# A two-layer hybrid block on one core: a fourth weight buffer in the feed-forward, the first mixer without GpSimd, the input also transposed, and an ending by token halves

## The chip, the cores and the metric

The kernel runs on one core of a Trainium2 chip. The metric is the device time in microseconds of one execution. "TensorE" is PE in the profile (PEld is its weight load), VectorE is DVE, ScalarE is ACT, GpSimd is POOL and SyncE is SP.

## The reference

256 tokens of width 2048 pass two layers. Each layer is a mixer and a gated feed-forward, both with a residual and with an RMS norm ahead of them; a last norm follows. Everything is float32.

```
for layer in range(2):
    if layer == 0: h = h + gdn_rglru_mixer(rmsnorm(h, ab_norm), ab_w_in, ...)   # gated delta rule heads + linear recurrence
    else:          h = h + fox_moba_mixer(rmsnorm(h, cd_norm), cd_w_in, ...)    # forgetting attention + block attention
    h = h + (silu(rmsnorm(h, ffn_norm) @ w_gate) * (rmsnorm(h, ffn_norm) @ w_up)) @ w_down   # 2048 -> 5632 -> 2048
return rmsnorm(h, final_norm)
```

In the first mixer `hn @ w_in` gives, for 8 heads of 128, q, k, v and z, two small gate vectors, and the two inputs of an LRU of 8 blocks. q, k, v pass a causal convolution of width 4 and SiLU. The gated delta rule works on chunks of 64 tokens and needs the inverse of a unit lower triangular matrix of each chunk.

## The kernel before

All weights stream once from HBM in units of 128 x 1024 float32 (512 KB). To keep float32 precision at the speed of the one-pass format, each unit is split into a high part (`whi`, a cast on ScalarE, L176) and a low part (`wlo`, a subtraction on VectorE, L177), and the activations `X` are kept as high and low too. A product takes three matmuls: high by high, high by low, low by high. `load` (L160) takes one of three raw buffers and issues the DMA on SyncE; `whi` has four buffers, `wlo` three. `split` (L171) works in steps of `step` columns: 512 in the mixers (`unit`'s default, two ScalarE and two VectorE operations for each unit), 1024 in the feed-forward.

`wstat` (L180) is a projection with the weights as the stationary operand: 2 units, 16 row groups of 128, result transposed (features on partitions); the plain form takes 48 matmuls of 256 columns. `xstat` (L214) has the activations stationary and 512 weight columns moving. `block` (L340) in the feed-forward does a 2 x 2 grid of such outputs, and one group of its row blocks by seven products instead of eight: `seven` loads b11, b12, b22 and b21 and makes sums T1 to T4 of them on VectorE (`total`, L303), so that some raw buffers stay occupied until two sums have read them. A block with four row groups has 12 plain units and 4 loads of this kind. `ffn` (L413) runs 11 gate/up blocks in pieces of 4, 4 and 3, and after each piece two down blocks that add into `h`. `turn` transposes the gated result.

Work beside the projections is written as generators (`tasks`): `tick` after each unit lets up to two of them take a step. So the delta rule's head tasks, the triangular inverse (`group_task`, L670) and the LRU run spread among the projections. The order of instructions on an engine follows the program order, but a tool that lays it out at build time may move ready instructions ahead.

The start: `h` comes in four pieces of 512 KB in natural layout (tokens on partitions), with the first weights between them. `to_x` (L252) transposes it by TensorE, 32 transposes, and ScalarE and VectorE write `X`. Then `mixer0` runs the projections of 8 heads (k, q, v order of the stored weights: L835 on), with the sums of squares of `h` (`sumsq`, L247) after the second tile; `ready` broadcasts the norm factor and starts the gates; the convolutions (`conv`, L490: one multiplication, one ScalarE scaling, three VectorE multiply-adds) follow each projection.

In the first mixer GpSimd does: `vg` (L616, 16 of 128x128), `dec` (L627, 8 of 128x256), the block mask `Cb` (L665, 16 of 128x128), the LRU's products (L559, 8 of 128x256; L578 and L588, 4 each of 128x512), the gating of `ly` (L878, 8 of 128x256), and two memsets. At the end (L1030) it multiplies four pieces by the final norm's weight.

In `group_task` the last step of the inverse works on two pairs of 32-row strips; each pair's result leaves at once:

```
            P2 = ms([128, 8, 32], "Pi4")
            for a, b in pairs:
                for m in range(8):
                    PE.matmul(P2[a, m], V1[b, m], Px[b, m, b], start=True, stop=True)
                V.tensor_scalar_mul(Px[a, :, b], P2[a], -1.0)
```

The end: the last block holds its last three units back, so that token half 0 finishes its matmuls before half 1 (`tail`). `h` is added for both halves, then `last` (L1009) computes the norm of each half, scales it in four pieces and issues four stores for each half on SyncE.

## Time and profile before

| | before |
|---|---|
| median of 3 runs | 2314.95 us (2314.65 to 2317.55) |
| the profiled execution | 2313.76 us |
| its span | 2312.0 us |
| mean granted TensorE clock | 0.997 |
| HBM read | 416.12 MB, mean 181 GB/s over the span |

A row of a stretch (a window) reads: from:to in us, its length, busy us (and number of instructions) of PE, PEld, DVE, ACT and POOL, the granted clock, the DMA engines' mean busy share, GB/s. With one tile's name only the engines that touch the tile are listed. A row of the timeline reads: start, length, engine, line, operation, written tile<-read tiles, size, and in brackets the idle time of the engine ahead of it and what ended it. A row of the groups ends with busy us and mean ns of one, then idle time ahead. A row of the waits reads: who <- for whom: us in total, times, longest. The profile writes some helper tiles short, for instance `F` for the four outputs of a block, `M` for the seven products, `Pi` for the inverse's.

Busy time of TensorE counts matmuls with modelled ends that overlap each other; a matmul of 512 columns is shown with some 0.39 us.

### The profile page before, as it was taken

Reading aid. Unit: us, or ns where it says so; the run is one execution under the profiler, and the core shown is the slowest. Engines: PE = TensorE matmul, PEld = TensorE weight load, DVE = VectorE, ACT = ScalarE, POOL = GpSimd, SP = SyncE. Lnnn points to the kernel's source line nnn. Section 1 sums busy time; section 2 is a strip of 40 time slices with the busy share of each in tenths; the row PEclk is TensorE's granted clock in tenths of the full one; section 3 lists DMA queues with packets and bytes.
Section 4 is the critical chain, followed back from the end, with each engine's and each line's share of the span. In section 5 each row is a group of like instructions: output and inputs, shape, how many; then the busy total and the mean of one; then the engine's idle time right before and its main releaser. Section 6 shows DMA issues by size and latency. Waiting matters only on the chain.

```text
span 2312.0 us, 31583 instructions
## 1 busy us (share of the span) xinstructions
PE 2268.1 (98%) x11630; PEld 1901.1 (82%) x11630; DVE 1824.4 (79%) x2840; ACT 1229.2 (53%) x1826; POOL 58.0 (3%) x74
## 2 busy tenths in 40 slices
PE   8999999999999999999999999999999999999997
PEld 8999888878878888888878888887888878888875
DVE  7898767788787888778876658867888788787888
ACT  7665654555444555455554445545554455554554
POOL 0211200000000000000000000000000000000000
PEclk9999999999999999999999999999999999999999
DMA  6444445566566556666555454555566566566564
GB/s 205 156 157 154 137 146 176 169 192 201 184 191 206 182 192 194 191 199 199 175 188 170 149 171 166 171 189 177 181 200 197 185 194 201 187 199 202 183 209 146
DMA packets 117356, 420.29 MB, mean 182 GB/s; under 512 B 12977, under 2 KB 14513, under 8 KB 117073
## 3 DMA queue, kind: packets, MB, share of 16 engines
q1 hardware_dynamic: 117200, 418.27, 56.0%
q8 instruction: 91, 1.49, 0.3%
q14 instruction: 65, 0.52, 0.1%
HBM read 416.12 MB, written 2.10 MB: 181 GB/s over the span
## 4 chain that ended last, share of the span: by engine, by line
PE 75%; DVE 12%; DMA 8%; ACT 3%; issue 1%; ACTq 0%; DVEq 0%; SPq 0%
PE F L336 13%; PE F L337 12%; PE F L335 12%; PE Pw L192 7%; PE Pw L197 6%; DVE wlo L177 5%; PE Px L237 4%; PE Px L238 4%; PE Px L239 4%; DMA raw<-in_gu 4%; DVE T L306 4%; DMA raw<-in_dn 3%; PE Pw L195 2%; PE Pw L196 2%; ACT whi L176 2%; PE M L337 1%
## 5 line engine op out<-in xcount | busy, mean ns | idle before, releaser
L176 ACT CAST whi<-raw 128x512 fp32r<-128x512 f32 (+1 forms) x1006 | 819.9, 832 | 771.8 <-DMA raw<-in_gu 217.8
L177 DVE TENSOR_TENSOR wlo<-raw,whi 128x512 fp32r<-128x512 f32 (+1 forms) x1006 | 943.7, 955 | 338.4 <-PE F L336 106.6
L336 PE MATMUL F<-wlo,X 128*128 128x512 f32 x1100 | 430.8, 392 | 8.6 <-DVE wlo L177 8.6
L335 PE MATMUL F<-whi,X 128*128 128x512 f32 x1100 | 428.5, 392 | 1.2 <-ACT whi L176 1.1
L337 PE MATMUL F<-whi,X 128*128 128x512 f32 x1100 | 428.5, 390 | 0.0
L197 PE MATMUL Pw<-X,wlo 128*128 128x256 f32 x1152 | 324.2, 282 | 0.0
L336 PEld LDWEIGHTS F<-wlo,X 128*128 128x128 f32 x1100 | 206.6, 188 | 58.3 <-DVE wlo L177 17.2
L335 PEld LDWEIGHTS F<-whi,X 128*128 128x128 f32 x1100 | 206.2, 188 | 44.2 <-ACT whi L176 2.6
L337 PEld LDWEIGHTS F<-whi,X 128*128 128x128 f32 x1100 | 206.5, 188 | 42.7
L192 PE MATMUL Pw<-X,whi 128*128 128x512 f32 x640 | 230.3, 403 | 0.0
L309 ACT CAST thi<-T 128x1024 fp32r<-128x1024 f32 x136 | 142.9, 1051 | 145.5 <-DVE T L306 145.4
L197 PEld LDWEIGHTS Pw<-X,wlo 128*128 128x128 f32 x1152 | 218.7, 190 | 0.4
L336 PE MATMUL F<-wlo,hid 128*128 128x512 f32 x536 | 210.1, 392 | 4.5 <-DVE wlo L177 4.3
L335 PE MATMUL F<-whi,hid 128*128 128x512 f32 x536 | 208.7, 392 | 1.0 <-ACT whi L176 0.9
L337 PE MATMUL F<-whi,hid 128*128 128x512 f32 x536 | 208.9, 390 | 0.0
L310 DVE TENSOR_TENSOR tlo<-T,thi 128x1024 fp32r<-128x1024 f32 x136 | 166.0, 1221 | 28.8 <-ACT thi L309 28.0
L195 PE MATMUL Pw<-X,whi 128*128 128x256 f32 x512 | 148.5, 290 | 0.0
L196 PE MATMUL Pw<-X,whi 128*128 128x256 f32 x512 | 144.9, 283 | 0.0
L192 PEld LDWEIGHTS Pw<-X,whi 128*128 128x128 f32 x640 | 120.2, 188 | 29.3 <-issue 0.7
L336 PEld LDWEIGHTS F<-wlo,hid 128*128 128x128 f32 x536 | 100.6, 188 | 29.7 <-DVE wlo L177 9.4
L335 PEld LDWEIGHTS F<-whi,hid 128*128 128x128 f32 x536 | 100.4, 188 | 22.4 <-ACT whi L176 2.1
L337 PEld LDWEIGHTS F<-whi,hid 128*128 128x128 f32 x536 | 100.6, 188 | 20.5
(357 smaller groups left out, 3217.8 us busy)
## 6 DMA issues: line engine op xcount, KB each, us to landing
raw<-in_gu SPq DMA_DIRECT2D x352, 512.0 KB, 4.2
raw<-in_dn SPq DMA_DIRECT2D x176, 512.0 KB, 4.2
raw<-in_w0w SPq DMA_DIRECT2D x80, 512.0 KB, 3.6
raw<-in_wo SPq DMA_DIRECT2D x64, 512.0 KB, 3.8
raw<-in_w1w SPq DMA_DIRECT2D x64, 512.0 KB, 3.6
raw<-in_w1x SPq DMA_DIRECT2D x32, 512.0 KB, 3.8
raw<-in_w0x SPq DMA_DIRECT2D x16, 512.0 KB, 3.6
h<-in_x SPq DMA_DIRECT2D x4, 512.0 KB, 6.5
```

The costliest lines, as they stand in the source:

```text
L176: S.copy(hi[:, s], raw[:, s])
L177: V.tensor_sub(lo[:, s], raw[:, s], hi[:, s].bitcast(F32))
L192: PE.matmul(P.rearrange("p a b -> p (a b)"), hi[:, kk], X[:, k].rearrange("p a b -> p (a b)"), start=k == 0, stop=False)
L195: PE.matmul(P[:, 0], hi[:, kk], X[:, k, 0], start=k == 0, stop=False)
L196: PE.matmul(P[:, 0], hi[:, kk], X[:, k, 1], start=False, stop=False)
L197: PE.matmul(P[:, 0], lo[:, kk], X[:, k, 0], start=False, stop=k == NK - 1)
L237: PE.matmul(Ps[t], x[:, 0, ts], hi[:, kk], start=k == 0, stop=False)
L309: S.copy(hi, t)
L310: V.tensor_sub(lo, t, hi.bitcast(F32))
L335: PE.matmul(self.t, xh, hi[:, kk], start=self.i == kk == 0, stop=False)
L336: PE.matmul(self.t, xh, lo[:, kk], start=False, stop=False)
L337: PE.matmul(self.t, xl, hi[:, kk], start=False, stop=kk == 1 and self.i == self.n - 1)
```

## The change

1. Feed-forward: every fourth call of `load` takes a buffer `raw4` of its own in the phase's pool, so that four raws rotate.
2. All splits are of 1024 columns.
3. The first mixer's GpSimd operations move to VectorE, the squares `a2` to ScalarE. The memsets stay.
4. The host also passes the input transposed (`xt`). `first` loads it in four quarters, makes `X` from it without TensorE, and runs the first three projections together, quarter by quarter, with weights loaded and split in halves of 512 columns. `h` itself is loaded only after head 1's first projection, where its squares, the norm factor and the LRU rate are computed. Eleven matmuls on zeros come first of all.
5. The convolutions of the first tiles are held in a list; from head 1's third projection on, two are done after each projection. The three outputs of head 0 stay in the PSUM tiles of `ms`.
6. In `group_task` the copies and the scaling of both pairs come after the matmuls of both.
7. At the end the token half 0 is added, normalised, scaled and stored before half 1 is added; three stores for each half (768, 512 and 768 columns), one of them on ScalarE's queue. The last multiplications are VectorE's.

```diff
+    loads, more = [0], []
...
+        more[:] = [] if mixer else [1]
...
-    nc.sync.dma_start(tab[:, 0:NTAB0], A["tab"][:, 0:NTAB0])
-    early = []
-    for g in range(4):
-        nc.sync.dma_start(h[:, :, g * 512:(g + 1) * 512], A["x"][:, :, g * 512:(g + 1) * 512])
...
+    nc.sync.dma_start(col[:, 0:16], A["col"][:, 0:16])
+
+    with tc.tile_pool(name="warm", bufs=1) as wp:
+        wz = wp.tile([128, 256], F32, name="wz")
+        V.memset(wz, 0.0)
+        S.activation(wz[:, 0:1], wz[:, 1:2], AF.Copy)
+        Pz = ms([128, 256], "Pz")
+        for _ in range(11):
+            PE.matmul(Pz, wz[:, 128:256], wz[:, 0:256], start=True, stop=True)
...
     def load(src):
-        if early:
-            return early.pop(0)
-        raw = wr.tile([128, 1024], F32, name="raw")
+        loads[0] += 1
+        if more and loads[0] % 4 == 0:
+            raw = mx.tile([128, 1024], F32, name="raw4", tag="raw4", bufs=1)
+        else:
+            raw = wr.tile([128, 1024], F32, name="raw")
         nc.sync.dma_start(raw, src)
         return raw
...
-        for i in range(0, 1024, step):
-            s = slice(i, i + step)
-            S.copy(hi[:, s], raw[:, s])
-            V.tensor_sub(lo[:, s], raw[:, s], hi[:, s].bitcast(F32))
+        S.copy(hi, raw)
+        V.tensor_sub(lo, raw, hi.bitcast(F32))
         return hi, lo
...
+    def first(srcs, w):
+
+        xt = ogp.tile([128, NK, T], F32, name="xt", tag="og")
+        Ps = [ms([128, T], "Pw") for _ in srcs]
+        for q in range(4):
+            ks, c = slice(4 * q, 4 * q + 4), slice(q % 2 * 512, q % 2 * 512 + 512)
+            nc.sync.dma_start(xt[:, ks], A["xt"][:, ks])
+            if q % 2 == 0:
+                ws = [(wr.tile([128, 1024], F32, name="raw"), wh.tile([128, 1024], F32R, name="whi"),
+                       wl.tile([128, 1024], F32R, name="wlo")) for _ in srcs]
+            for i, (raw, _, _) in enumerate(ws):
+                nc.sync.dma_start(raw[:, c], srcs[i][q // 2][:, c])
+            if q == 0:
+                nc.sync.dma_start(tab[:, 0:NTAB0], A["tab"][:, 0:NTAB0])
+                nc.sync.dma_start(col[:, 16:], A["col"][:, 16:])
+            for k in range(4 * q, 4 * q + 4):
+                S.activation(X[:, k, 0], xt[:, k], AF.Copy, scale=w[:, k:k + 1])
+                V.scalar_tensor_tensor(out=X[:, k, 1], in0=xt[:, k], scalar=w[:, k:k + 1], in1=X[:, k, 0].bitcast(F32),
+                                       op0=ALU.mult, op1=ALU.subtract)
+            for P, (raw, hi, lo) in zip(Ps, ws):
+                S.copy(hi[:, c], raw[:, c])
+                V.tensor_sub(lo[:, c], raw[:, c], hi[:, c].bitcast(F32))
...
-            G.tensor_tensor(out=XI[:, n], in0=XI[:, n], in1=xc, op=ALU.mult)
+            V.tensor_tensor(out=XI[:, n], in0=XI[:, n], in1=xc, op=ALU.mult)
...
-                    G.tensor_tensor(out=a2, in0=R[:, n:n + 2], in1=R[:, n:n + 2], op=ALU.mult)
+                    S.activation(a2, R[:, n:n + 2], AF.Square)
...
             for a, b in pairs:
                 for m in range(8):
                     PE.matmul(P2[a, m], V1[b, m], Px[b, m, b], start=True, stop=True)
+            for a, b in pairs:
                 V.tensor_scalar_mul(Px[a, :, b], P2[a], -1.0)
...
+        def convs(n):
+
+            for hd, which, P in [waiting.pop(0) for _ in waiting[:n]]:
+                c = head_conv(hd, (1, 0, 2)[which], P, [q[:, which] for q in qks[hd]] if which < 2 else None)
+                if which == 2:
+                    start(head_task(hd, qks[hd], c))
...
+            if hd == 0:
+                waiting += [(0, i, P) for i, P in enumerate(first([W[16 + i] for i in range(3)], cl["n0"]))]
+                continue
+            for which in range(3):
+                early = hd == 1 and which < 2
+                waiting.append((hd, which, wstat(W[16 + 3 * hd + which], mid=ready if early and which else None)))
+                if early and which == 0:
+                    for g in range(4):
+                        nc.sync.dma_start(h[:, :, g * 512:(g + 1) * 512], A["x"][:, :, g * 512:(g + 1) * 512])
+                        sumsq(g)
+                    nc.sync.dma_start(tab[:, NTAB0:], A["tab"][:, NTAB0:])
+                    rstd()
+                    start(lru_rate())
+                    continue
+                convs(2)
...
+                    if end and fin:
+                        fin(t)
...
+    def second_half(t):
+        o = fo[0][:, t]
+        for g in (2, 3):
+            sumsq(g, t)
+            V.tensor_tensor(out=o[:, cs[g]], in0=h[:, t, cs[g]], in1=fo[0][:, 2, cs[g]], op=ALU.mult)
...
+        a, b, c = (slice(0, 512), slice(512, 1280), slice(1280, D))
+        S.activation(o[:, a], o[:, a], AF.Copy, scale=y)
+        for q in (b, c):
+            V.tensor_scalar_mul(o[:, q], o[:, q], y)
+        for q, eng in ((b, nc.sync), (a, nc.scalar), (c, nc.sync)):
+            eng.dma_start(out[:, t, q], o[:, q])
```

More of the change, by code (lines that the diff above doesn't have):

```diff
@@ L359, in seven @@
             b11 = load(src(0, 2 * m))
-            M[0].add(q(0, 0), split(b11, 1024))
+            M[0].add(q(0, 0), split(b11))
             yield
@@ L366, in seven @@
             b22 = load(src(1, 2 * m + 1))
-            F[0][1].add(cx(3), split(b22, 1024))
+            F[0][1].add(cx(3), split(b22))
             yield
@@ L374, in seven @@
             b21 = load(src(0, 2 * m + 1))
-            F[0][0].add(q(1, 0), split(b21, 1024))
+            F[0][0].add(q(1, 0), split(b21))
             yield
@@ L411, in block, with ffn @@
         return [[y.t for y in f] for f in F], e
-    def ffn(L, then, tail=0):
+    def ffn(L, then, fin=None):
         gu, dn = A[f"gu{L}"], A[f"dn{L}"]
@@ L452, in ffn @@
                 F, e = block(lambda i, u: dn[2 * p + i, u0 + u], lambda k: hid[:, k], {0: lambda: ch[0]}, piece,
-                             {2: turn, 3: turn} if todo else {}, tail if end else 0)
+                             {2: turn, 3: turn} if todo else {}, 3 if end and fin else 0)
                 hs = [[h[:, t, (2 * p + i) * 512:(2 * p + i + 1) * 512] for i in range(2)] for t in range(2)]
@@ L460, in ffn @@
                         V.tensor_tensor(out=hs[t][i], in0=F[t][i], in1=e[t][i], op=ALU.add)
-                if b == NB:
+                    if end and fin:
+                        fin(t)
+                if b == NB and not (end and fin):
                     then(2 * p)
@@ L731, in group_task @@
                     PE.matmul(P1[b, m], C[a, m, b], Xi[a, m], start=True, stop=True)
+            for _, b in pairs:
                 S.copy(V1[b], P1[b])
@@ L996, in body @@
     with phase(True):
-        for g in range(4):
-            start(to_x(g, cl["n0"]))
-        finish()
         mixer0()
@@ new lines, in first_half @@
+            fo.append(res.tile([128, 3, D], F32, name="fin", tag="X"))
+            nc.sync.dma_start(fo[0][:, 2], A["fw"].to_broadcast([128, D]))
+        sumsq(g)
+        for t in range(2):
+            V.tensor_tensor(out=fo[0][:, t, cs[g]], in0=h[:, t, cs[g]], in1=fo[0][:, 2, cs[g]], op=ALU.mult)
+        if g == 1:
+            V.tensor_reduce(out=part, in_=ssp[:, :, 0:2], axis=AX.X, op=ALU.add)
+            V.tensor_scalar(out=part, in0=part, scalar1=1.0 / D, scalar2=EPS, op0=ALU.mult, op1=ALU.add)
+            S.activation(pre, part, AF.Sqrt)
```

109 lines of the change are left out of this document (35 added, 74 removed).

## The prediction

> **What bounds the kernel now.** I read the page first: busy time by engine, then the chain that ended last. After it came the busy time by stretch, the waits, and the timeline around the longest gaps of TensorE.
>
> ```profile
> PE 2268.1 (98%) x11630; PEld 1901.1 (82%) x11630; DVE 1824.4 (79%) x2840; ACT 1229.2 (53%) x1826; POOL 58.0 (3%) x74
> PE 75%; DVE 12%; DMA 8%; ACT 3%; issue 1%; ACTq 0%; DVEq 0%; SPq 0%
> 450.00:1130.00 680.00, 671.33 (x2984) 549.54 (x2984) 556.10 (x585) 350.04 (x369) 0.00 (x0) 1.00 0.60 192
> 1585.00:2300.00 715.00, 704.78 (x3115) 574.16 (x3113) 587.81 (x615) 368.11 (x391) 2.36 (x2) 1.00 0.60 191
> L336 PEld LDWEIGHTS F<-wlo,X 128*128 128x128 f32 x1100 | 206.6, 188 | 58.3 <-DVE wlo L177 17.2
> ```
>
> TensorE holds 75% of the chain, so only its idle time can be won; the number of weight matmuls does not change. Busy time overstates TensorE: matmuls overlap. The weight loads (PEld) measure better. In the dense run below two matmuls of 512 columns start 0.22 to 0.23 us apart and each load takes 0.19 us, so a dense feed-forward would show PEld at about 83% (0.188/0.227). The two feed-forward rows show 80.8% and 80.3%: about 17 and 23 us of 1395 us are lost.
>
> Where they go is seen in one typical place (ScalarE, VectorE, TensorE from the timeline; then waits, the last of SyncE's queue):
>
> ```profile
> 550.41 1.05 ACT L176 CAST whi<-raw 128x1024 fp32r<-128x1024 f32 x1 [0.79 <-DMA raw<-in_gu]
> 551.50 1.22 DVE L177 TENSOR_TENSOR wlo<-raw,whi 128x1024 fp32r<-128x1024 f32 x1 [0.62 <-ACT whi L176]
> 556.64 1.22 DVE L177 TENSOR_TENSOR wlo<-raw,whi 128x1024 fp32r<-128x1024 f32 x1
> 556.74 0.39 PE L335 MATMUL F<-whi,X 128*128 128x512 f32 x1
> 556.96 0.39 PE L335 MATMUL M<-thi,comb 128*128 128x512 f32 x1
> 557.91 0.50 PE L336 MATMUL F<-wlo,X 128*128 128x512 f32 x1 [0.56 <-DVE wlo L177]
> PEld F L336 <- DVE wlo L177: 27.3, 35, 1.4
> ACT whi L176 <- DMA raw<-in_gu: 107.4, 93, 2.4
> SPq L164 <- DVE wlo L177: 1482.9, 595, 8.5
> ```
>
> At 557.91 TensorE is 0.73 us late (0.95 us after its predecessor instead of 0.22) for `wlo`. VectorE worked without a pause from 551.50 on, but before that it had waited 0.62 us for the cast, and the cast 0.79 us for a load. The load could not be issued sooner, because SyncE waits for a raw buffer (1482.9 us in 595 waits). So three raw buffers are the first cause, and VectorE's burst is the second. All such waits of the weight loads come to 27.3 us in 35 waits.
>
> **The change part by part.** The profiled execution took 2313.76 us around a span of 2312.0; the median of the runs is 2314.95, 1.2 us above it. I sum against the execution and add 1.2.
>
> *Fourth raw buffer.* Counting the loads, the fourth falls on plain units in every block of four row groups (12 plain units and 4 loads of the combined part, 16 in all), never on the raws that stay occupied for the sums T. So it always rotates quickly. A load is issued one buffer earlier, which covers the 0.79 and 0.62 us above, more than the 0.73 us lost. But where VectorE is late by itself nothing is won, and the first blocks after a mixer wait for other things. Ends: 0 and -27.3. I take half, **-14**, because the ACT and DVE pauses before the gap are of the gap's size. A loss is possible only if the new buffer's memory frees late at the entry of the feed-forward; that stays in the range.
>
> *Pi4 in one piece.* TensorE runs half of L737, then must wait for VectorE's L738 of the first pair, although the two halves use different data:
>
> ```profile
> 286.18 0.69 PE L737 MATMUL Pi<-gsc,V 32*32 32x32 f32 x16
> 292.36 0.40 DVE L738 TENSOR_SCALAR gsc<-Pi 32x256 f32<-32x256 f32 x1
> 292.91 1.03 PE L737 MATMUL Pi<-gsc,V 32*32 32x32 f32 x16 [4.91 <-DVE gsc L738]
> 290.80:297.60 6.80, 4.69 (x25) 3.88 (x26) 5.71 (x11) 0.00 (x0) 0.00 (x0) 0.50 0.48 154
> 282.95 1.29 POOL L588 TENSOR_TENSOR lsc<-lsc,HS 128x512 f32<-128x512 f32 x1
> 283.05 1.22 DVE L100 TENSOR_TENSOR rq4c<-rq4b 128x8 f32<-128x8 f32 x1
> 285.22 0.16 DVE L100 TENSOR_TENSOR rq4c<-rq4b 128x8 f32<-128x8 f32 x1
> ```
>
> The wait costs 4.91 us. The row from 290.80 to 297.60 shows the granted clock at 0.50, so the 3.7 us of work after 293.9 took twice its time: 1.9 us more. With all 32 matmuls ahead of L738 nothing of the pair waits for VectorE: **-6.8**. VectorE was late there partly through GpSimd: the same L100 takes 1.22 us beside L588 on POOL and 0.16 us without it. That goes too. What is late next is the `wlo` of the following unit; it could leave up to 3 us of the wait, so the ends are -6.8 and -3.
>
> The clock is the place where a rule weighs in. The Trainium skill ("TensorE: Matmul & The Clock Gate", Part 1) says an idle window of about 3.4 us halves the clock until a busy window has passed; the row above agrees (idle from 288, 0.50 from 290.80). By that rule any new gap of this length costs some 3.4 us beyond itself.
>
> *The start.* It loses 16 small transposes of pairs (32 matmuls) and gains 2 MB of transposed input, while `h` is loaded later, behind the first tile of head 1.
>
> ```profile
> 5.78 8.29 SPq L164 DMA_DIRECT2D raw<-in_w0w  x2
> 0.00:30.55 30.55, 19.14 (x144) 17.95 (x144) 0.00 (x0) 0.00 (x0) 1.00 0.73 248
> 0.00:48.15 48.15, 31.27 (x240) 29.70 (x241) 1.69 (x4) 0.00 (x0) 1.00 0.63 213
> 42.00:48.00 6.00, 6.00 (x51) 5.83 (x50) 5.86 (x17) 4.53 (x9) 0.00 (x0) 1.00 0.27 87
> 0.00:12.00 12.00, 4.79 (x22) 3.63 (x22) 4.29 (x10) 6.46 (x13) 2.03 (x6) 1.00 0.81 262
> L554 PE MATMUL Pgate<-cv,lw 128*128 128x256 f32 x16 | 5.1, 399 | 0.0
> 35.02 1.52 DVE L500 SCALAR_TENSOR_TENSOR cv<-cx,col,cv 128x255 f32<-128x255 f32 x3 [0.48 <-ACT cv L496]
> ```
>
> The rows with the matmuls of `Pw` alone say that the first three tiles end at 30.55 us and the first five at 48.15. A tile has 48 matmuls, and in the dense row from 42 to 48 one takes 6.00/51 = 0.12 us, so a tile takes 5.8 us. After the change the first three tiles need 2.1 MB of input, 3.1 MB of weights and 0.2 MB of tables; at the 262 GB/s of the row 0 to 12 that is 20.6 us, plus some 3 us of issue and first landing. The warm-up's 22 half-passes of at most 0.40 us (L554) end by 10 us, about when the first split weights arrive, and cost nothing. The weights of the third quarter wait on SyncE until VectorE has freed the raws of the first, with all later loads queued behind them; at 0.42 to 0.6 us an operation that is at 13 to 15 us, and they land before TensorE gets there at some 17.6. So the third tile ends near 26. Tile four lasts to 32. Behind its 1 MB come 2.1 MB of `h` and 0.4 MB of table before tile five. By the whole sum of 9.5 MB at 262 GB/s its first half lands at 37; at full DMA share (262/0.81 = 323 GB/s) at 31. ScalarE's squares of `h` stand ahead of tile five's casts and wait for `h`, but the weights land behind `h` anyway. I take 35 with the cast, a gap of 3 us, then tile five to 41, and the small projection that lies before 48.15 in the row (16.4 us of work for two tiles and 17.6 us of time, so 4.9 us of it) to 46. That is 2 us earlier. The six convolutions held back (1.52 us of L500 and 0.42 of L493 each, 11.6 us of VectorE) then come two at a time, 3.9 us per 5.8 us of TensorE beside 2.4 us of splits, 6.3 against 5.8 in five steps; I charge 1 us. Net **-1**; ends -6 (no gap) and +6 (late landing, half clock).
>
> One sentence from a page: the Trainium skill ("DMA: Bandwidth & Descriptors", Rules for kernel authors) wants at least 1 MiB in a transfer, where the start now moves weights in pieces of 256 KB; no run here shows their rate.
>
> *First mixer without GpSimd, 1024-column splits.*
>
> ```profile
> 120.00:160.00 40.00, 40.00 (x332) 39.79 (x331) 38.30 (x141) 26.30 (x55) 5.30 (x8) 1.00 0.48 152
> 60.00:120.00 60.00, 60.00 (x495) 59.54 (x494) 51.64 (x167) 40.68 (x86) 16.93 (x24) 1.00 0.48 157
> L493 DVE TENSOR_TENSOR cx<-Pw,rb 128x256 f32<-128x256 f32 x32 | 13.4, 419 | 8.0 <-PE Pw L197 7.0 <-ACT rb L282 0.9
> L953 DVE TENSOR_SCALAR pr<-pr,sxx 128x128 f32<-128x128 f32 x16 | 4.4, 275 | 0.0
> L457 DVE TENSOR_TENSOR e<-h,e 128x512 f32<-128x512 f32 x48 | 31.2, 684 | 0.0
> 17.27 3.09 DVE L177 TENSOR_TENSOR wlo<-raw,whi 128x512 fp32r<-128x512 f32 x5
> 2292.15 2.35 DVE L177 TENSOR_TENSOR wlo<-raw,whi 128x1024 fp32r<-128x1024 f32 x2
> ```
>
> VectorE gets 32 operations of 128x128 (0.275), 24 of 128x256 (0.42) and 4 of 128x512 (0.68): 8.8 + 10.1 + 2.7 = 21.6 us; ScalarE gets four squares. A pair of 512-column splits takes 2 x 3.09/5 = 1.24 us, one of 1024 takes 2.35/2 = 1.18: 0.06 us saved in each of 128 units, 8 us. VectorE further regains what POOL stretched, between nothing and the 53 us that POOL works in this mixer (58.0 less 5.0 at the end); I take 15. So VectorE's load hardly changes, and since TensorE has no idle in the rows from 60 to 160, nothing can be won there: **0**, ends 0 and +6, the loss where VectorE already has 38.30 of 40 us. In the other mixer the splits change nothing that TensorE waits for.
>
> *The end by token halves.*
>
> ```profile
> 2298.93 0.39 PE L337 MATMUL F<-whi,hid 128*128 128x512 f32 x1
> 2300.11 0.68 DVE L460 TENSOR_TENSOR h<-F,e 128x512 f32<-128x512 f32 x1
> 2300.71 0.70 DVE L1033 SCALAR_TENSOR_TENSOR fin<-fin,fin 128x1 f32<-128x1 f32 x1
> 2303.87 4.48 SPq L1045 DMA_DIRECT2D out_h<-fin  x8
> 2304.54 0.88 DVE L1044 TENSOR_SCALAR fin<-fin,fin 128x512 f32<-128x512 f32 x2
> ```
>
> After TensorE's last matmul 13 us pass. The first token half waits for the second: the eight stores start at 2303.87 and their issues alone last 4.48 us. After the change the first half's stores leave early and three issues follow the last scaling, two of them at once on two queues: 4.48 us become some 1.5, -3. VectorE has four multiplications of 0.68 us more (they were POOL's) and loses the stretched 0.70 and the like: +1. **-2**, ends -4 and +1.
>
> Sum: -14 - 6.8 - 1 + 0 - 2 = -23.8; 2313.76 - 23.8 + 1.2 = **2291 us**. The measurement tells about 0.2%, 4.6 us, from no change.
>
> **The rivals.** (a) *VectorE's burst is the bound of the feed-forward*, and a load that lands earlier only waits longer. For it: VectorE works without a pause from 551.50 to 557.9. Against it: the pauses just before. Only about 3 us are then won: 2302.
> (b) *The late `h` opens a gap of 5 us* before tile five, and the clock falls to half as at 290.80 for 6.8 us, at 3.4 us of loss: the start becomes +5 instead of -1, the total 2297. For it: 2.5 MB in one queue ahead of the weights. Against it: TensorE is fed at 1 MB per 5.8 us, less than the DMA can do.
> (c) *Slower: VectorE becomes the bound of the first mixer.* It has 38.30 of 40 us at 120 to 160; if POOL's work is added there and nothing is regained, the 21.6 us and the 11.6 us of held convolutions reach TensorE: +33 against -23.8, 2324. It decides from 24 us of exposed VectorE work. Against it: 51.64 of 60 before that place, and the L100 rows, which show that POOL's work is not free for VectorE now.
> (d) *The change does not do what it says*: the order in which the instructions are laid out at build time, not the source, decides; the pair of L737 then waits elsewhere and the fourth buffer waits for memory at each entry: 2315.
>
> **How the numbers follow.** Forecast 0.45, (a) 0.17, (b) 0.20, (c) 0.12, (d) 0.06. Faster by over 0.2%: the first three, 0.82; within: (d), 0.06; slower: (c), 0.12. The range reaches down to 2277 (feed-forward -22, start -6) and up to 2312 (a with the start's loss), leaving (c) and (d) out.
>
> **What would show it.** Right: no wait of TensorE at L737's successor and no 0.50 clock near 290; the waits of F's `wlo` loads at half of 27.3 us or less; ACT's waits for `in_gu` well below 107.4 us per feed-forward; three tiles of `Pw` done by 26 to 27 us and five by about 41; less than 11.5 us after the last matmul. Wrong: PEld in the feed-forward still at 80.5%, TensorE gaps between 45 and 200 us behind `wlo` (then c), or a gap above 3 us near 33 us with the clock at 0.50 (then b).

## The result, and the profile after

| | before | after |
|---|---|---|
| median | 2314.8 us (4 runs, 2313.19 to 2317.55) | 2286.09 us (4 runs, 2284.92 to 2287.37) |
| the profiled execution, its span | 2313.76 us, 2312.0 us | 2286.04 us, 2284.2 us |

The ratio is 0.9875, 95% interval 0.9858 to 0.9892: 28.7 us faster. The forecast was 2291 us, range 2277 to 2312.

In the two traces I cut the span at the last matmul of the narrow `Pw` tiles (the 1,152nd) and at the first and last matmul of `F` in each feed-forward:

| stretch, us | before | after | difference | forecast |
|---|---|---|---|---|
| start to the last narrow tile | 176.4 | 178.7 | +2.3 | -1 |
| rest of the first mixer | 274.1 | 265.5 | -8.6 | -6.8 and 0 |
| first feed-forward | 722.8 | 713.5 | -9.3 | |
| second mixer | 401.6 | 401.4 | -0.2 | 0 |
| second feed-forward | 724.0 | 713.3 | -10.7 | both: -14 |
| behind the last matmul of `F` | 13.0 | 11.8 | -1.2 | -2 |

The ends of the feed-forwards can be read from the rows of the tile `F` (count, least/median/longest ns, start of the first and of the last); the first feed-forward before, and then after:

```profile
L335 PE MATMUL F<-whi,X x550: 388/389/499, 450.5 to 1107.0; 128*128 128x512 f32 x184
L337 PE MATMUL F<-whi,hid x268: 387/389/481, 628.8 to 1173.3; 128*128 128x512 f32 x134
```

```profile
L366 PE MATMUL F<-whi,X x550: 387/389/796, 444.2 to 1091.5; 128*128 128x512 f32 x184
L368 PE MATMUL F<-whi,hid x268: 389/389/478, 622.4 to 1157.7; 128*128 128x512 f32 x134
```

Busy time and the chain from the page after, and the two feed-forward windows:

```profile
PE 2259.0 (99%) x11620; PEld 1906.7 (83%) x11620; DVE 1805.0 (79%) x2655; ACT 1205.9 (53%) x1580; POOL 2.0 (0%) x6
PE 97%; DVE 1%; DMA 1%; ACT 1%; issue 0%; DVEq 0%; ACTq 0%; SPq 0%
```

```profile
450.00:1130.00 680.00, 678.84 (x3030) 561.46 (x3031) 564.74 (x596) 355.93 (x378) 0.00 (x0) 1.00 0.60 196
1585.00:2270.00 685.00, 684.14 (x3059) 565.48 (x3058) 568.66 (x603) 353.73 (x375) 0.00 (x0) 1.00 0.59 194
```

TensorE's share of the chain rose from 75% to 97%. PEld in the feed-forwards is at 82.6% (561.46/680 and 565.48/685), against 80.8% and 80.3% before and the 83% that the prediction worked out for a dense run. GpSimd has nothing left but the memsets. The waits, all of the span:

```profile
ACT whi L174 <- PE F L368: 424.1, 279, 3.0
ACT whi L174 <- DMA raw<-in_gu: 86.1, 60, 3.6
PEld F L366 <- ACT whi L174: 7.1, 4, 2.9
```

Before, ScalarE's casts waited for loads, over the whole span:

```profile
ACT whi L176 <- DMA raw<-in_gu: 217.8, 188, 3.0
```

(The 107.4 us that the prediction shows are those of one window, from 450 to 1130 us.) Now the casts mostly wait for TensorE to free a `whi`: the loads run ahead and all `whi` buffers are full. The wait of F's loads for `wlo` (27.3 us in 35 waits) is gone from the list. In its place stand four waits for `whi`, all at the entries of the two feed-forwards. The first of them, in the waits of SyncE's queue, the timeline of ScalarE and TensorE, and a window:

```profile
SPq L168 <- ACT junk L281: 6.4, 1, 6.4
```

```profile
449.48 2.94 ACT L174 CAST whi<-raw 128x1024 fp32r<-128x1024 f32 x3 [2.15 <-DMA raw<-in_gu]
450.57 0.73 PE L366 MATMUL F<-whi,X 128*128 128x512 f32 x2 [2.47 <-ACT whi L174]
```

```profile
451.82:455.23 3.41, 3.04 (x8) 2.18 (x8) 3.41 (x5) 2.49 (x3) 0.00 (x0) 0.50 0.59 175
```

The fourth raw buffer lies on memory that the mixer's `junk` still uses. Its first load waits 6.4 us on SyncE with all later loads behind it, TensorE stands for `whi`, and the granted clock is then 0.50 for 3.41 us. The start has a like case, here in the same three views and with the rows of `Pw` alone at the end:

```profile
SPq L211 <- PE Pz L90: 4.5, 1, 4.5
```

```profile
10.23 1.29 SPq L211 DMA_DIRECT2D xt<-in_xt  x3
14.04 4.11 ACT L221 ACTIVATE X<-xt,col 128x256 fp32r<-128x256 f32 x10 [2.45 <-DMA xt<-in_xt]
14.60 0.56 PE L229 MATMUL Pw<-X,whi 128*128 128x256 f32 x2 [4.46 <-ACT X L221]
```

```profile
14.91:18.32 3.41, 3.41 (x17) 3.20 (x16) 3.41 (x10) 3.41 (x10) 0.00 (x0) 0.50 0.98 356
0.00:33.65 33.65, 19.05 (x144) 18.83 (x145) 0.00 (x0) 0.00 (x0) 0.95 0.82 285
0.00:45.17 45.17, 30.57 (x240) 30.30 (x240) 0.00 (x0) 0.00 (x0) 0.96 0.79 274
```

The input tile `xt` takes over the memory of the closed pool that held the warm-up's operand, so its load waits 4.5 us for the warm-up matmuls `Pz`. TensorE, warmed for this moment, stands 4.46 us until 14.60 us, and its clock is at half from 14.91 to 18.32 us. Three tiles of `Pw` end at 33.65 us (before 30.55), five at 45.17 (48.15).

### The profile page after: what moved, and what is told of

It is laid out like the page before. It is cut to its first block, busy times and chain, and to the rows that moved or that the text cites. A ratio compares the mean times of both kernels' runs of the same rounds, so it can differ in the third digit from the quotient of the medians.

```text
span 2284.2 us, 31143 instructions
## 1 busy us (share of the span) xinstructions
PE 2259.0 (99%) x11620; PEld 1906.7 (83%) x11620; DVE 1805.0 (79%) x2655; ACT 1205.9 (53%) x1580; POOL 2.0 (0%) x6
## 4 chain that ended last, share of the span: by engine, by line
PE 97%; DVE 1%; DMA 1%; ACT 1%; issue 0%; DVEq 0%; ACTq 0%; SPq 0%
PE F L366 17%; PE F L368 17%; PE F L367 17%; PE Pw L194 7%; PE Pw L199 6%; PE Px L268 5%; PE Px L270 4%; PE Px L269 4%; PE M L367 3%; PE M L368 3%; PE M L366 3%; PE Pw L197 2%; PE Pw L198 2%; PE Ph L453 1%; PE Psc L975 1%; DVE wlo L175 0%
## 5 line engine op out<-in xcount | busy, mean ns | idle before, releaser
L174 ACT CAST whi<-raw 128x1024 fp32r<-128x1024 f32 x744 | 779.9, 1052 | 889.1 <-PE F L368 424.1
L175 DVE TENSOR_TENSOR wlo<-raw,whi 128x1024 fp32r<-128x1024 f32 x744 | 906.1, 1222 | 329.5 <-PE F L367 141.9
L199 PE MATMUL Pw<-X,wlo 128*128 128x256 f32 x1104 | 310.2, 281 | 0.0
L199 PEld LDWEIGHTS Pw<-X,wlo 128*128 128x128 f32 x1104 | 209.5, 190 | 0.2
L197 PE MATMUL Pw<-X,whi 128*128 128x256 f32 x464 | 135.0, 291 | 0.0
L198 PE MATMUL Pw<-X,whi 128*128 128x256 f32 x464 | 131.4, 283 | 0.0
```

The source lines that it names most:

```text
L174: S.copy(hi, raw)
L175: V.tensor_sub(lo, raw, hi.bitcast(F32))
L197: PE.matmul(P[:, 0], hi[:, kk], X[:, k, 0], start=k == 0, stop=False)
L198: PE.matmul(P[:, 0], hi[:, kk], X[:, k, 1], start=False, stop=False)
L199: PE.matmul(P[:, 0], lo[:, kk], X[:, k, 0], start=False, stop=k == NK - 1)
```

## The experiments

Each kernel was timed in turn with the kernel before on the same chip; that kernel's median was 2316.7 us beside e1 to e4, 2315.13 beside e5 to e8, 2321.02 beside e9 to e12. So kernels of different groups compare within some 6 us, by the ratio no better than by the median: by the ratio e10 would be 5 us faster than the changed kernel, while its span is 3.5 us longer. Smaller differences are read from the stretches of the traces, cut as above, one trace for each kernel. Where programs agree, the rest of the first mixer comes out at 265.5 us every time, but the start lies between 178.2 and 179.4 us, and a feed-forward between 712.6 and 715.2.

| | median us | ratio to before, 95% | start | first mixer | ffn | ffn | behind | span |
|---|---|---|---|---|---|---|---|---|
| changed kernel | 2286.09 | 0.9875 (0.9858 to 0.9892) | 178.7 | 265.5 | 713.5 | 713.3 | 11.8 | 2284.2 |
| e1 three raws | 2309.35 | 0.9968 (0.9957 to 0.9980) | 178.3 | 265.5 | 724.4 | 725.5 | 12.1 | 2307.2 |
| e2 pair loops apart | 2289.42 | 0.9883 (0.9869 to 0.9896) | 178.2 | 267.3 | 714.0 | 714.2 | 11.9 | 2287.1 |
| e3 pairs and GpSimd | 2295.96 | 0.9909 (0.9894 to 0.9924) | 178.9 | 273.7 | 713.6 | 714.5 | 11.8 | 2294.0 |
| e4 warm-up constant | 2283.5 | 0.9856 (0.9842 to 0.9869) | 174.8 | 265.5 | 713.5 | 713.5 | 11.3 | 2280.1 |
| e5 buffer in early memory | 2281.62 | 0.9850 (0.9835 to 0.9865) | 179.4 | 265.5 | 710.9 | 710.2 | 11.8 | 2279.4 |
| e6 e4 and e5 | 2278.55 | 0.9835 (0.9821 to 0.9850) | 175.8 | 265.5 | 712.1 | 710.7 | 11.3 | 2277.5 |
| e7 one warm-up matmul | 2284.05 | 0.9864 (0.9846 to 0.9883) | 177.1 | 265.5 | 713.0 | 713.5 | 11.6 | 2282.1 |
| e8 before, with the buffer | 2293.41 | 0.9901 (0.9886 to 0.9916) | 176.3 | 273.9 | 714.9 | 712.3 | 12.4 | 2291.0 |
| e9 GpSimd back | 2289.95 | 0.9867 (0.9852 to 0.9882) | 179.0 | 267.2 | 715.2 | 712.6 | 11.7 | 2287.7 |
| e10 end together | 2287.44 | 0.9853 (0.9836 to 0.9870) | 178.9 | 265.5 | 715.1 | 714.9 | 11.9 | 2287.7 |
| e11 buffer on other loads | 2278.13 | 0.9814 (0.9800 to 0.9829) | 178.5 | 265.5 | 710.1 | 709.0 | 11.8 | 2276.5 |
| e12 later first use, and e4 | 2275.32 | 0.9802 (0.9788 to 0.9817) | 174.6 | 265.5 | 709.4 | 709.4 | 11.8 | 2272.1 |

**The fourth buffer alone: taken away (e1), and added to the kernel before (e8).**

```
-        more[:] = [] if mixer else [1]        # e1: the changed kernel
+        more[:] = []
```

> The changed kernel with three raw buffers in the feed-forwards again; all else as changed. By the two traces the feed-forward stretches (first feed-forward matmul to the mixer behind it, and to the last matmul) became 9.4 and 10.8 us shorter. Theory A, the fourth buffer did that: 18 to 21 us slower than the changed kernel, 2304 to 2307, and the waits of the weight loads of F for wlo come back to about 27 us. Rival B, VectorE's burst was the bound and the other edits (VectorE without GpSimd beside it, the smaller start) did it: no more than 3 us slower, 2286 to 2289. Rival C, the buffer did it but its late memory at each entry takes 4 to 5 us back: then the stretches lose over 20 us without it and the entry gap of F behind whi (2.85 and 2.69 us now) goes.

> The kernel before with one part of the change alone: the fourth raw buffer in the feed-forwards. Theory A, the buffer by itself brings what the feed-forwards gained: 18 to 21 us faster than before, 2294 to 2297. Rival B, VectorE's burst was the bound: 0 to 3 us faster, 2312 to 2315. Rival C, it works only together with the other edits: in between, the rest missing when all else is undone.

Waits of e1, then of e8:

```profile
ACT whi L174 <- DMA raw<-in_gu: 231.4, 200, 3.2
PEld F L367 <- DVE wlo L175: 27.7, 35, 1.2
```

```profile
ACT whi L182 <- PE F L343: 421.8, 283, 3.0
```

Both agree with theory A, a little above its 18 to 21 us. Without the buffer the feed-forwards are back at 724.4 and 725.5 us and the wait for `wlo` at 27.7 us in 35 waits; the kernel is 2316.7 - 2309.35 = 7.4 us faster than the one before beside it, where the changed kernel is 28.7 us faster, so 21.3 us are gone. In the kernel before the buffer alone gives 21.7 us (2315.13 to 2293.41) and the waits of the changed kernel. VectorE's burst is no bound of itself: with a load ready ahead, the same subtractions are in time. Rival C of e1 holds as well: its stretches lose 23.1 us, the entry's gap is gone, and the gain without the entry's loss is larger, as e12 shows. Away from the entry, from the 64th to the 2,048th matmul of F and M, the first feed-forward takes 467.7 us in e1 and 457.2 in the changed kernel.

**What the pair's wait in the first mixer is made of (e2, e3, e9).** e2 puts the copies and the scaling back into the pair loops, e9 the first mixer's elementwise operations on GpSimd, e3 both:

```
             for a, b in pairs:                                  # e2 and e3
                 ...PE.matmul(P2[a, m], V1[b, m], Px[b, m, b])...
-            for a, b in pairs:
                 V.tensor_scalar_mul(Px[a, :, b], P2[a], -1.0)
```
```
-            V.tensor_tensor(out=XI[:, n], in0=XI[:, n], in1=xc, op=ALU.mult)     # e3 and e9, and six others
+            G.tensor_tensor(out=XI[:, n], in0=XI[:, n], in1=xc, op=ALU.mult)
```

> The changed kernel with the pair loops of the first mixer's state update as before: the scaled copies and the scaling back lie inside the loop over pairs again, so the second pair's matmuls of Pi stand behind VectorE's scaling of the first. GpSimd stays out of the mixer. Theory A, the wait belongs to the order of the pairs: a gap of about 5 us near 285 us and the clock at half behind it come back, 5 to 7 us slower than the changed kernel, 2291 to 2293. Rival B, VectorE was late there through what GpSimd did beside it (1.22 us instead of 0.16 us in one operation): without GpSimd the gap is under 1.5 us and the time within 1.5 us of the changed kernel, 2285 to 2288.

> The changed kernel with both undone: the first mixer's elementwise operations on GpSimd again, and the pair loops as before. Theory A, the order of the pairs makes the wait: as much slower as with the pair loops alone, 5 to 7 us. Theory B, it takes both, a late VectorE and the order: 5 to 9 us slower, 2291 to 2295, while the pair loops alone cost under 1.5 us. Rival C, the 8.6 us that this stretch gained come from the 1024-column splits: then under 3 us slower, 2286 to 2289.

> The changed kernel with the first mixer's elementwise operations on GpSimd again; the pairs of the state update stay in one piece. Apart, the pair loops cost 1.8 us between the last narrow tile and the feed-forward (traces: 267.3 against 265.5 us), and pair loops with GpSimd 8.2 us (273.7). Theory A, what the prediction says: the pair's wait is made by the order alone, so with the pairs in one piece GpSimd costs under 1.5 us, 2286 to 2288 on the scale of the changed kernel's 2286.1, and the two need each other to cost 8.2. Rival B, GpSimd delays VectorE and this shows with or without the pair loops: the whole rest, 4 to 7 us slower, 2290 to 2293, with waits of TensorE for VectorE between 180 and 350 us.

Against the 265.5 us of the changed kernel, the pair loops alone cost 1.8 us, GpSimd alone 1.7, and both 8.2; before it was 274.1. So the wait needed both, and little is left for the 1024-column splits and the held convolutions together (274.1 - 273.7 = 0.4 us); neither was tried alone. That is theory B of e3. In e2 the truth lies between the theories, nearer to B: 1.8 us in this stretch, 3.3 by the medians. The timeline of e3 shows how the two meet (GpSimd, then VectorE), and below it TensorE's wait:

```profile
285.03 5.05 POOL L621 TENSOR_TENSOR lsc<-lsc,HS 128x512 f32<-128x512 f32 x4 [3.96 <-ACT HS L617]
285.15 1.27 DVE L103 SCALAR_TENSOR_TENSOR rq4b<-rq4c,rq4b 128x8 f32<-128x8 f32 x1
286.45 1.21 DVE L101 TENSOR_TENSOR rq4c<-rq4b 128x8 f32<-128x8 f32 x1
287.69 1.19 DVE L102 SCALAR_TENSOR_TENSOR rq4c<-rq4c,sso 128x8 f32<-128x8 f32 x1
288.92 1.18 DVE L103 SCALAR_TENSOR_TENSOR rq4b<-rq4c,rq4b 128x8 f32<-128x8 f32 x1
290.13 0.17 DVE L101 TENSOR_TENSOR rq4c<-rq4b 128x8 f32<-128x8 f32 x1
```

```profile
PE Pi L770 <- DVE gsc L771: 4.6, 1, 4.6
```

GpSimd's four products run from 285.03 to 290.08, and exactly so long each of VectorE's four small operations takes 1.2 us in place of 0.17: 4.2 us late, and behind them on VectorE stands the scaling that the second pair waits for. In the trace the products end at 286.39, 287.63, 288.86 and 290.08, and the small operations at 286.42, 287.66, 288.88 and 290.10: here a small operation lasted until the product beside it was done. The wait is not the whole cost: TensorE stands from 287.93 us on, and its clock falls during the wait.

```profile
289.49:296.32 6.83, 3.77 (x23) 3.16 (x24) 5.43 (x16) 0.00 (x0) 0.58 (x1) 0.50 0.01 2
```

The 3.77 us of work in this row at half clock cost some 1.9 us more. The Trainium skill ("GPSIMD Engine Reference", 8. Key points) says that GpSimd shares its interfaces to SBUF with VectorE, and that VectorE's instructions with two inputs in SBUF contend with it; these rows agree, at 1.2 us for 0.17. In e9 the same four operations are stretched (L103 at 284.19 takes 1.25 us), but with the pairs in one piece TensorE has other work, and only 1.7 us remain. That is close to theory A of e9, which had under 1.5, and far from B's 4 to 7. Matched matmul by matmul with the changed kernel, e9 falls behind at two places alone, by 0.84 and 0.90 us, where it has two small waits:

```profile
PE Py L792 <- DVE gsc L773: 0.6, 1, 0.6
PEld Px L269 <- DVE wlo L175: 0.9, 1, 0.9
```

Matched in the same way, e2 falls behind by 0.95 us at the inverse of the first group of heads (190 to 201 us) and by 0.89 at that of the second (280 to 288), and nowhere else. Its waits of TensorE for VectorE are no longer than those of the changed kernel; what differs there is that TensorE runs the matmuls of each step in two halves with other matmuls between (16 matmuls of `Pi` take 0.69 us, all 32 in one piece 1.09). Why the halves cost this much is not shown further. In e3 the same comparison gives 1.0 us at the first inverse and 7.2 at the second, about the sum of the wait (4.6), the half clock (1.9) and the halves (0.9).

**The start (e4, e7).**

```
-    with tc.tile_pool(name="warm", bufs=1) as wp:     # e4
-        wz = wp.tile([128, 256], F32, name="wz")
+        wz = cst.tile([128, 256], F32, name="wz")
```
```
-        for _ in range(11):                           # e7
+        for _ in range(1):
```

> The changed kernel with the operand of the warm-up matmuls in the pool of constants, which is never freed, in place of a pool whose memory the first input tile takes over; nothing else differs in the source. In the changed kernel's trace the first input load waits 4.5 us on SyncE for the warm-up matmuls, lands at 13.93 us, and TensorE then stands 4.7 us and has its clock at half from 14.91 to 18.32 us. Theory A, this wait is why the third tile of Pw ends at 33.5 us instead of the 26 us of the forecast: the load leaves some 4.5 us earlier, the gap and the half clock go, 5 to 8 us faster than the changed kernel, 2278 to 2281. Rival B, the start is bound by the bytes that the loads bring: the first matmul starts earlier but the third tile of Pw ends less than 2 us earlier, 2284 to 2286. Rival C, the layout made at build time changes by it and something else comes late: slower.

> The changed kernel with one warm-up matmul in place of eleven. Theory A, the wait of the first input load for the warm-up matmuls costs the start its time: the load leaves some 4 us earlier. Whether the whole gets faster hangs on the clock: in the changed kernel's trace the clock is full from 8.08 us on and then at half again from 14.91 to 18.32 us, so the warm-up gains nothing there now; without it TensorE starts at half clock for some 3.4 us of its work, as it does now. So 3 to 5 us faster than the changed kernel, 2281 to 2283. Rival B, the warm-up is needed or the bytes bound the start: within 1.5 us or slower, 2285 or more.

The timeline of e4 (SyncE, then VectorE and TensorE at tile five) and its rows of `Pw`:

```profile
1.19 0.42 SPq L211 DMA_DIRECT2D xt<-in_xt  x1
34.75 0.46 PE L311 MATMUL Prb<-dg,tab 128*128 128x128 f32 x2 [1.65 <-issue]
34.76 1.22 DVE L175 TENSOR_TENSOR wlo<-raw,whi 128x1024 fp32r<-128x1024 f32 x1
```

```profile
0.00:26.93 26.93, 17.46 (x145) 17.46 (x146) 0.00 (x0) 0.00 (x0) 1.00 0.88 300
0.00:41.65 41.65, 29.73 (x241) 29.15 (x241) 0.42 (x1) 0.00 (x0) 1.00 0.84 288
```

The load of `xt` leaves at 1.19 us instead of 10.23, the half clock is gone, and three tiles end 6.7 us earlier, at 26.93 us. At tile five 3 us of this are given back (five tiles 3.5 us earlier): `h` is now late there. Its last piece lands at 30.26 us, the table at 31.27, and tile five's first weights behind them in the same queue at 32.56; their cast ends at 33.69. VectorE waits for the squares of `h` until 31.71 and works out the norm factor first, so that their `wlo` and TensorE's `Prb` start only at some 34.75, where TensorE has stood for 1.65 us. This is the chain of rival (b), in its place, at 3 us and without a half clock. The whole start gains 3.9 us (178.7 to 174.8; the median 2.6): theory A in kind, below its 5 to 8 us in size, which forgot the next limit. In e7 the load is early too (3.53 us), but the clock is at half until 15.46 us (matmuls of 256 columns start 0.21 us apart before, 0.12 behind); the start ends at 177.1, and the whole is 2.0 us faster by the medians, between its two theories. So eleven warm-up matmuls are worth 177.1 - 174.8 = 2.3 us where no load waits for them, and cost 178.7 - 177.1 = 1.6 us where one does; both are differences of single traces, and the start scatters by about 1 us.

**The entry of the feed-forward (e5, e6, e11, e12).** e5 gives the fourth buffer a pool of its own, opened first; e6 adds e4's edit. e11 begins the count of loads three higher. e12 has e4's edit and a later first use:

```
-            raw = mx.tile([128, 1024], F32, name="raw4", tag="raw4", bufs=1)     # e5, e6
+            raw = r4.tile([128, 1024], F32, name="raw4")
```
```
-    loads, more = [0], []                                       # e11
+    loads, more = [3], []
```
```
-        more[:] = [] if mixer else [1]                          # e12
+        more[:] = [] if mixer else [loads[0] + 4]
...
-        if more and loads[0] % 4 == 0:
+        if more and loads[0] > more[0] and loads[0] % 4 == 0:
```

> The changed kernel with the fourth raw buffer in a pool of its own, opened first in a feed-forward, so that it lies on memory that the mixer has freed early; nothing else differs. In the changed kernel's trace the load into it waits on SyncE at both entries (6.4 us behind ScalarE's junk, 4.9 us behind the matmuls of Px), TensorE then stands 2.85 and 2.69 us for whi with 2 us of small gaps, and its clock is at half for 3.41 us. Theory A, the late memory makes these gaps: 5 to 8 us faster than the changed kernel, 2278 to 2281, half of it at each entry. Rival B, the entry waits for something else anyway (X, the raws of the mixer): under 1.5 us, 2285 to 2287.

> The changed kernel with both mends: the warm-up operand in the pool of constants, and the fourth raw buffer in early freed memory. If both theories hold the two gains add, since they lie in different stages: 10 to 16 us faster than the changed kernel, 2270 to 2276. If neither holds it is within 2 us of it.

> The changed kernel with the count of loads begun three higher, so that the fourth raw buffer falls on other loads: in each block on the raws of the combined part, which stay occupied for the sums T, and on plain units between them, in place of plain units alone. Theory A, the buffer helps only because it rotates quickly (a step of the prediction): 5 to 12 us slower than the changed kernel, 2291 to 2298, and the waits of the weight loads of F for wlo come back in part. Rival B, any fourth buffer will do, since one of the others comes free in its place: within 1.5 us, or faster by up to 4 us if the first use at each entry moves off the late memory.

> The changed kernel with the warm-up operand in the pool of constants, and the fourth raw buffer first used at the eighth load of a feed-forward in place of the fourth. With three raws throughout, the traces have the 16th matmul of F and M at 4.67 us after the first one, with the fourth buffer from the fourth load on at 8.85 us, and with that buffer in an early freed pool at 7.02 us. Theory A, the late memory alone makes the difference, and a later first use avoids it: some 4 us at each entry besides the 3 to 4 us of the start, 2274 to 2277, faster than with both mends of before (2278.6). Rival B, the fourth buffer is needed at once, and the first blocks lose by its absence what the entry gains (with three raws the 96th matmul comes at 26.1 us, with four at 28.0): 2278 to 2281.

The counter of `load` also runs through the 122 weight loads of the first mixer (74, 16 and 32 of three weight tensors). So the new buffer's first use in a feed-forward is the second load in the changed kernel, the third in e11 and the sixth in e12, where the expectation of e12 counts the fourth and the eighth; what each run tests stays the same. In a block of four row groups the buffer takes plain units alone in the changed kernel, and b11, b22, b21 and one plain unit in e11.

e5 shortens the feed-forwards by 2.6 and 3.1 us, in sum at the low end of theory A; by the medians it gains 4.5 us, since its start drew a half-clock spell of 6.83 us and ends at 179.4. Its memory is free earlier, but not at once: the load now waits on SyncE for the mixer's last projection, and TensorE waits 1.3 us for `whi` at the first entry in place of 2.8.

```profile
SPq L170 <- PE Px L272: 4.9, 1, 4.9
```

```profile
PE F L368 <- ACT whi L176: 1.3, 2, 0.9
```

e6 gains 7.5 us by the medians, less than the 10 to 16 forecast, since both parts were smaller, and in its trace the clock still falls for 3.41 us at the first entry. e11 was meant to show that the buffer must rotate quickly; it shows the opposite, rival B, by more than the 4 us that B allowed. Its span is 7.7 us shorter than the changed kernel's, 3.4 and 4.3 us of it in the feed-forwards. From the 64th to the 2,048th matmul of F and M its first feed-forward takes 457.2 us, the same as the changed kernel's: on which loads the buffer falls makes no difference in the steady run, and all of the gain is the entry's. e12 takes that gain on purpose and is the fastest of all: 2275.32 us, inside theory A's 2274 to 2277. That is 45.7 us below the kernel before beside it, which was slow in that group (2321.02); by the spans it is 39.9 us below the kernel before and 12.1 us below the changed kernel. Its windows (the two feed-forwards, then the span from 8.29 us to near the end):

```profile
445.00:1130.00 685.00, 684.24 (x3068) 566.46 (x3067) 572.73 (x610) 361.74 (x388) 0.00 (x0) 1.00 0.62 197
1555.00:2260.00 705.00, 703.10 (x3140) 581.04 (x3139) 589.63 (x631) 366.62 (x392) 0.00 (x0) 1.00 0.62 195
8.29:2264.50 2256.21, 2248.38 (x11607) 1900.40 (x11606) 1800.54 (x2643) 1200.33 (x1570) 0.00 (x0) 1.00 0.59 185
```

The clock does not fall between 8.29 and 2264.50 us. Its feed-forwards are 709.4 us each: the fourth buffer is worth 15.0 and 16.1 us there (e1: 724.4 and 725.5), of which the changed kernel gave back 4.1 and 3.9 at the entries.

**The end (e10).**

```
-                    if end and fin:        # inside the loop over t, behind the add of one half
-                        fin(t)
+                if end and fin:            # behind both halves
+                    for t in range(2):
+                        fin(t)
```

> The changed kernel with the end's order undone in one point: both token halves are added to h before either is normalized and stored, so the first half again waits for the second. Theory A, ending by halves brings what the last matmul's tail became shorter by (13.05 to 11.84 us): 1 to 2 us slower than the changed kernel, 2287 to 2288. Rival B, the tail is set by the second half's own chain, and the shorter tail comes from GpSimd's absence and the stores' two queues: within 0.5 us.

The last matmul, the first store and the last store, after and then e10:

```profile
2272.40 0.39 PE L368 MATMUL F<-whi,hid 128*128 128x512 f32 x1
2276.04 3.13 SPq L1077 DMA_DIRECT2D out_h<-fin  x4
2278.42 0.34 ACTq L1077 DMA_DIRECT2D out_h<-fin  x1
```

```profile
2275.77 0.39 PE L368 MATMUL F<-whi,hid 128*128 128x512 f32 x1
2279.57 3.02 SPq L1078 DMA_DIRECT2D out_h<-fin  x4
2281.51 0.34 ACTq L1078 DMA_DIRECT2D out_h<-fin  x1
```

Rival B holds for the end: the stretch is 11.9 against 11.8 us, and the last store on ScalarE's queue leaves 5.74 us after the last matmul against 6.02. The median alone (2287.44) would fit theory A as well, but the trace has nearly all of e10's longer span in the feed-forwards, 1.6 us in each, which the last section explains. The first half's stores leave only 3.64 us after the last matmul even in the changed kernel, because on VectorE the second half's additions (2272.68 and 2274.06) stand ahead of the first half's scaling (2275.40). In these traces the end follows the time at which the first store leaves: 4.94 us after the last matmul before, 3.64 after the change, 3.80 in e10. From there to the last landing pass 6.84 us with eight issues on one queue, and 6.74 and 6.71 (e10) with six on two. The DMA engines are busy most of this time with the same 2.1 MB (before, then after):

```profile
2304.80:2310.60 5.80, 0.00 (x0) 0.00 (x0) 0.62 (x2) 1.11 (x2) 0.00 (x0) 0.50 0.96 358
2276.80:2282.20 5.40, 0.00 (x0) 0.00 (x0) 1.79 (x6) 0.77 (x2) 0.00 (x0) 0.61 1.01 386
```

So fewer issues on two queues gave next to nothing. Which edit lets the first store leave earlier was not tried alone; e8, with the end as before, has 12.4 in place of 13.0, so part of the 1.2 us is scatter.

## Why the prediction came out right

The whole was 5 us off (2291 against 2286.09): by the stretches, the feed-forwards gave 6.0 us more than forecast and the first mixer 1.8 more, while the start gave 3.3 less and the end 0.8 less. Another 1.1 us is the 1.2 added for the median, which lies 0.05 us above the profiled execution here. The errors partly cancel, so that a total within 5 us is partly luck; the mechanism that carries most of the gain was the right one. Two of the signs that the prediction named did not come: the times of the tiles, and less than 11.5 us after the last matmul (11.84). Its range has small slips: by the terms that it names, the ends are 2278 and 2309, not 2277 and 2312.

- **Fourth raw buffer: mechanism right, term mis-sized.** I took -14, half of 27.3, for the bursts of VectorE that a load cannot help. The runs give -20.0 in the two stretches, and -31.1 from e1 to e12, more than my end of -27.3: the quoted wait counts only the weight loads of F for `wlo`, and the trace before has 6.1 us more of them for `whi` (9 waits). The pauses of ScalarE and VectorE before the gap were the cause, and rival (a) is out. "A loss is possible only if the new buffer's memory frees late at the entry" stood in the text without a price; that happened, at 4 us for each entry. The argument that the buffer must fall on plain units, to rotate quickly, was not needed (e11).
- **Pi4 in one piece and the mixer without GpSimd: sum a little small, shares wrong.** -6.8 and 0 against -8.6 in this stretch. A wait of 4.9 us and the half clock behind it did go. I gave all of the pair's wait to the order of the matmuls and gave GpSimd only a remark ("partly through GpSimd"). Each edit by itself leaves only 1.7 or 1.8 us of the 8.2: either one removes most of it. Rival (c) did not come: VectorE's busy time fell from 1824.4 to 1805.0 us with GpSimd's work added. The row from 287.00 on has the clock at 1.00, where 0.50 stood:

```profile
287.00:297.60 10.60, 10.60 (x56) 9.02 (x55) 10.60 (x16) 5.17 (x7) 0.00 (x0) 1.00 0.45 149
```

- **The start: the step that failed.** I had the third tile near 26 us, a gap of 3 us at tile five, five tiles at 41, net -1. The change gave 33.65 and 45.17 and +2.3. The failed sentence is that the warm-up "costs nothing": it was priced by TensorE's time alone, and not by the memory that its operand hands on to the first load. With that one tile moved (e4) the rows are 26.93, a 3 us gap and 41.65, and the stretch is 1.6 us shorter than before (176.4 to 174.8). The sum of bytes was sound (26.93 against "near 26"); what was missed was a dependence.
- **The end: too much.** -2 against -1.2, and not by the halves: e10 without them is 0.1 us longer. I priced the issues of the stores (4.48 us to some 1.5), while the transfer of their bytes sets the time from the first store on, 6.84 and 6.74 us. And I let the first half's stores leave early without asking what VectorE does in between.
- **Rival (d)** has one true clause, that the fourth buffer waits for memory at each entry; the rest of it did not happen.

## What to carry to other kernels

When a buffer is added, price its memory as well as its count: ask who used those bytes last, and place its first use behind that release; here a later first use and one constant moved to memory of its own took another 12.1 us off the span (e12). When two late things meet in one wait, undo each alone before giving it to either. A gap that is closed shows the next limit of the same stage, so the gain of a mend is bounded by what stands right behind it (tile five in e4).

## What the runs showed of the hardware

Between the first full clock and the last matmul, every half-clock spell in these traces lasts 3.41 us or twice that, and the same wait can draw either. At the first entry TensorE stood 2.47 us in the changed kernel and 2.56 us in e10, for the same load; the spell was 3.41 us in the one (the row from 451.82 above) and 6.83 in the other, in e10's timeline and window:

```profile
450.82 0.73 PE L366 MATMUL F<-whi,X 128*128 128x512 f32 x2 [2.56 <-ACT whi L174]
```

```profile
451.62:458.45 6.83, 6.53 (x15) 4.78 (x16) 6.38 (x7) 3.99 (x5) 0.00 (x0) 0.50 0.65 223
```

So the feed-forwards of programs that are the same there differ by 1.6 us from profile to profile (713.5 and 715.1). The Trainium skill ("TensorE: Matmul & The Clock Gate", Part 1) has a window of 3413 ns that runs free of the kernel, which agrees with these lengths; it has the clock fall after an idle window of about 3.4 us, and there these traces differ. In the wait that the prediction shows, TensorE is idle from 288.00 us and the clock is at half from 290.80, 2.8 us later, which is less than that window, though the prediction says that the row agrees. In e3 it falls 1.6 us into the wait (287.93 to 289.49). In e6 waits of 1.05, 0.22 and 0.44 us with matmuls between were enough:

```profile
446.26 0.73 PE L368 MATMUL F<-whi,X 128*128 128x512 f32 x2 [1.05 <-ACT whi L176]
448.34:451.75 3.41, 3.41 (x9) 2.67 (x10) 3.41 (x5) 1.64 (x2) 0.00 (x0) 0.50 0.52 166
```

In e5 waits of 0.90, 0.21 and 0.45 us at the same place were not, nor was the wait of 1.65 us at tile five in e4. So the length of the longest wait does not decide by itself; what does is not shown here.
